# Another order of the second block's projections and another hand-written plan of turns

## The chip, the cores and the metric

The kernel runs on one core of one Trainium2 chip. The metric is the device time of one execution, in microseconds (us). A run of the kernel before takes 1793.36 us (median of three, 1793.31 to 1794.03).

## The reference

Input x is 256 tokens of 1024 float32 values. The first block is two layers, each of a half-weighted SwiGLU feed-forward, a hybrid mixer (gated convolution and a gated linear recurrence) and another feed-forward, with layer norms. It is not touched. The second block is this, cut to what matters (`_hgrn2` is a gated linear recurrence of 4 heads of 128, `_dsa_attention` an attention of 8 heads of 64):

```python
h = _rms(x, norm1_g) * (1 + sc1) + sh1
z = h @ w_in
rq, rf, ri, rg, aq, ak, av, iq, ik, iw = jnp.split(z, IN_OFFSETS, axis=-1)
rec = _hgrn2(rq, rf, ri, rg, lb, rec_out_g)
aq, ak = _rms(aq by head, q_norm_g), _rms(ak by head, k_norm_g)
ik = _layernorm(ik, idx_k_norm_g, idx_k_norm_b)
att = _rms(_dsa_attention(aq, ak, av, iq, ik, iw, rel_bias), attn_out_g)
x = x + g1 * (concatenate([rec, att]) @ w_out)
x = x + g2 * _hier_moe(...)
```

In the attention, each query's 64 best keys are selected by an index score, the sum over 8 index heads of iw * relu(iq . ik), and only these keys (of admissible chunks) enter the softmax, with a relative position bias.

## The kernel before, in words

**Weights.** All weights come from memory as 1 MB blocks, each of two halves of 128x1024 float32. ScalarE casts a half to a high part (L195) and VectorE subtracts to get the low part (L196); TensorE multiplies in three products, high by high, high by low and low by high. So each half costs one instruction on ScalarE and one on VectorE before TensorE can take it. There are six split buffers. `spend` (L257) is called after each half: it releases the half, lets the next one be split and calls `tick`. At most three halves are split ahead of the one in use.

**Projections.** The loop over `ZSEQ` (L32) makes z piece by piece. RF, RQ and IQ (forget gates, recurrence queries, index queries) are four halves of 24 matmuls with 256 columns (L317 to L319), IK (index keys and index weights) is one such half. AK, RG, AV and RI (attention keys, recurrence gate, attention values, recurrence values) are four halves of 12 matmuls with 512 columns (L348). AQ is made ahead of the loop. The order before is RF, RQ, IK, IQ, AK, RG, AV, RI.

**Everything else in between.** The rest of the block's first part is written as Python generators in three queues. `tick` (L251) takes the next entry of `PLAN` (L34): its three digits say how many steps are taken from each queue at that point. There are two ticks in a half (one in the middle, one at its end), some before the loop, and after the loop `tick` goes on until the second queue is empty, then three output halves follow with three ticks each. A step issues instructions to all engines; each engine runs its own in order, so a step issued early stands ahead of the splits issued later on the same engine.
- First queue: `prepare` (constants, the bounds of the forget gate, L952), `index_keys` (norm and transposition of the index keys), `index_scores` (L985: six chunks of scores, then eight rounds that take the eight largest values each, L1010 and L1011, then a threshold, L1013), and `attention` (L1159).
- Second queue: `decay` (L1016, forget gates and running sums), `levels` (L1078) and `recurrence` (L1107).
- Third queue: `qk_norm` (L1141): square sums, then a multiply by the root for each of four tiles and for the two query tiles a multiply by the gain on GpSimd (L1151), then transposes.

`levels` works through seven distances: `level_in` (L1055) subtracts running sums (L1068, L1070, on VectorE or GpSimd by the bits of `LVS`), takes the exponential on ScalarE and multiplies (L1075 by the bits of `LVD`, L1076 on VectorE); `merge_level` (L1032) makes two tiles of matmuls (L1037) and VectorE copies them under a mask (L1038), which gives their PSUM bank back. Two buffers (`kd`, `qd`) take turns over the levels, so a level's input waits for the merge two levels before. `across` (L1041) is the last input, followed by a cross block (A01).

`attention` loads the bias as two 512 KB transfers on GpSimd's queue (L1166), the first into the buffer of aq, the second into that of iq; it adds the threshold result to it (`bias`), and for each head makes logits (L1192), a maximum and exponentials, transposes of the weights with copies (`values`, L1207) and products with the values (L1212 to L1214). Its norm ends in transposes (L957) after a multiply (L1252).

PSUM: `mm_tile` gives one of four banks in turn. When the projection named by `ATT_AT` (L33) begins, `attention` is queued and two of the four become its output banks; from then on two are left for everything else. `acc` banks are separate.

**Turns before, by the plan.** Scans of the forget gates come in RQ, the levels from IK to RG (the last merge and the cross block at RG's first half), scores in AK and RG, seven of the eight selection rounds at one turn in RG (digit 7 of "702"), square sums and norms in RG, transposes of queries and keys in AV, the bias from RI's first half, most of attention in RI and behind it.

Of the kernel before, what the change touches and what calls it, by code (L numbers as in the profile page):

```python
# [28 lines left out]
NSTAG = 5  # L29
OFF_B, OFF_C, OFF_V, OFF_XR, OFF_YR, OFF_G = 0, 1024, 2048, 3072, 4096, 5120  # L30
Z_RQ, Z_RF, Z_RI, Z_RG, Z_AQ, Z_AK, Z_AV, Z_IQ, Z_IK = 0, 512, 1024, 1536, 2048, 2560, 3072, 3584, 4096
ZSEQ = (Z_RF, Z_RQ, Z_IK, Z_IQ, Z_AK, Z_RG, Z_AV, Z_RI)  # L32
ATT_AT = Z_RI  # L33
PLAN = (  # L34
# [3 lines left out]
).split()  # L38
LAG_V, LAG_P = 1, 3
LVS = 161  # L40
# [28 lines left out]
BIG = 99.0  # L69
# [10 lines left out]
def weight_order():  # L80
# [42 lines left out]
    order.extend(("zt", Z_AQ, q) for q in range(4))  # L123
    for o in ZSEQ:
        if o == Z_IK:
# [99 lines left out]
def kernel(ctx, tc, x, blocks, vecs, lnrows, consts, rows, bias_w, wr, out):  # L225
# [675 lines left out]
    def t4(shape, dt=F32, name="t4"):  # L901
        return p2.tile(shape, dt, tag="t4", bufs=4, name=name)
# [256 lines left out]
    def attention(mix, oa):  # L1159
# [4 lines left out]
        for i in range(2):  # L1164
            b = t4([128, 4, 256], name="braw")
            nc.gpsimd.dma_start(b, bass.AP(tensor=scr.tensor, offset=scr.offset + 2048 * i + 127,  # L1166
                                           ap=[[4095, 128], [512, 4], [1, 256]]))
            braw.append(b)

        def bias(h):  # L1170
            b = braw[h // 4][:, h % 4]
            bm = p2.tile([128, 384], F32, tag="bm", bufs=2, name="bm")
            eng = nc.vector if BSD >> h & 1 else nc.gpsimd
            eng.tensor_add(bm[:, 0:128], b[:, 128:256], idx[:, 0:128])
            eng.tensor_add(bm[:, 128:384], b, idx[:, 128:384])
            bts[h] = bm
# [112 lines left out]
    ready = set()  # L1289
    for off in ZSEQ:  # L1290
        if off == ATT_AT:
            turn_[1] = False
            oa = [o_tile("oatt") for _ in range(2)]
            bg.append(attention(mix, oa))
# [520 lines left out]
```

## Time and profile before

| what | us |
|---|---|
| median of the runs | 1793.36 |
| the profiled execution, its own time | 1794.38 |
| its span in the trace | 1792.5 |
| TensorE busy | 1722.5 (96%) |
| VectorE busy | 1340.1 (75%) |
| ScalarE busy | 1036.5 (58%) |
| GpSimd busy | 62.0 (3%) |

The span is from the first to the last recorded instruction; 1.9 us of the profiled execution lie around it. Its mean granted TensorE clock is 0.991 of full speed. Times in rows are us from the start of the span unless they are marked ns. "Busy" counts instructions in execution; shares are averages over very different stages. The projections of the second block's loop run from 1298.7 us on; at 1448.4 us the part after them begins.

### The profile page before, as it was taken

Reading aid. Unit: us, or ns where it says so; the run is one execution under the profiler, and the core shown is the slowest. Engines: PE = TensorE matmul, PEld = TensorE weight load, DVE = VectorE, ACT = ScalarE, POOL = GpSimd, SP = SyncE. Lnnn points to the kernel's source line nnn. Section 1 sums busy time; section 2 is a strip of 40 time slices with the busy share of each in tenths; the row PEclk is TensorE's granted clock in tenths of the full one; section 3 lists DMA queues with packets and bytes.
Section 4 is the critical chain, followed back from the end, with each engine's and each line's share of the span. In section 5 each row is a group of like instructions: output and inputs, shape, how many; then the busy total and the mean of one; then the engine's idle time right before and its main releaser. Section 6 shows DMA issues by size and latency. Waiting matters only on the chain. (4 is left out here: it accounts for less than half of the span.)

```text
span 1792.5 us, 25724 instructions
## 1 busy us (share of the span) xinstructions
PE 1722.5 (96%) x10089; PEld 1501.5 (84%) x10089; DVE 1340.1 (75%) x1913; ACT 1036.5 (58%) x1500; POOL 62.0 (3%) x74
## 2 busy tenths in 40 slices
PE   7999999999999999999999998999899879999998
PEld 6888799999788878887999997888698667877876
DVE  5777878756767786778787557566778778998996
ACT  5655575644555555555756444555466547777774
POOL 0000000000000000000000000000114120000000
PEclk9999999999999999999999999999999989999999
DMA  8566645554557665666455545655352357988983
GB/s 321 206 252 246 233 171 185 188 192 161 223 208 260 239 244 188 250 246 246 176 188 185 187 169 202 244 190 180 119 188 92 126 197 294 352 315 332 348 317 131
DMA packets 56384, 394.12 MB, mean 220 GB/s; under 512 B 6424, under 2 KB 6728, under 8 KB 9920
## 3 DMA queue, kind: packets, MB, share of 16 engines
q1 hardware_dynamic: 52416, 375.94, 56.9%
q0 software_dynamic: 3264, 15.74, 2.6%
q8 instruction: 81, 1.33, 0.3%
q10 hardware_dynamic: 576, 0.74, 0.1%
q14 instruction: 47, 0.39, 0.1%
HBM read 391.30 MB, written 3.19 MB: 220 GB/s over the span
## 5 line engine op out<-in xcount | busy, mean ns | idle before, releaser
L196 DVE TENSOR_TENSOR split<-raw,split 128x1024 fp32r<-128x1024 f32 x611 | 735.7, 1226 | 260.0 <-ACT split L195 257.6
L195 ACT CAST split<-raw 128x1024 fp32r<-128x1024 f32 x611 | 627.9, 1048 | 99.1 <-PE acc L384 54.2
L329 PE MATMUL mmo<-xT,split 128*128 128x512 f32 x640 | 230.0, 399 | 0.0
L329 PE MATMUL mm<-xT,split 128*128 128x512 f32 x640 | 229.3, 398 | 0.0
L384 PE MATMUL acc<-split,ht 128*128 128x512 f32 x816 | 199.5, 392 | 4.1 <-ACT ht L311 3.5
L1544 PE MATMUL hp<-split,xg 128*128 128x512 f32 x768 | 187.7, 398 | 0.8 <-DVE split L196 0.8
L384 PEld LDWEIGHTS acc<-split,ht 128*128 128x128 f32 x816 | 147.9, 188 | 38.7 <-ACT ht L311 4.8
L330 PE MATMUL mmo<-xT,split 128*128 128x256 f32 x640 | 179.7, 281 | 0.0
L330 PE MATMUL mm<-xT,split 128*128 128x256 f32 x640 | 179.6, 281 | 0.0
L1544 PEld LDWEIGHTS hp<-split,xg 128*128 128x128 f32 x768 | 142.9, 188 | 34.7 <-DVE split L196 1.1
L317 PE MATMUL mm<-xT,split 128*128 128x256 f32 x600 | 169.9, 283 | 0.0
L319 PE MATMUL mm<-xT,split 128*128 128x256 f32 x600 | 169.8, 283 | 0.0
L318 PE MATMUL mm<-xT,split 128*128 128x256 f32 x600 | 169.8, 283 | 0.0
L329 PEld LDWEIGHTS mmo<-xT,split 128*128 128x128 f32 x640 | 120.3, 188 | 29.6
L329 PEld LDWEIGHTS mm<-xT,split 128*128 128x128 f32 x640 | 120.2, 188 | 29.1
L330 PEld LDWEIGHTS mm<-xT,split 128*128 128x128 f32 x640 | 120.8, 189 | 2.0
L330 PEld LDWEIGHTS mmo<-xT,split 128*128 128x128 f32 x640 | 120.9, 189 | 0.7
L317 PEld LDWEIGHTS mm<-xT,split 128*128 128x128 f32 x600 | 115.1, 192 | 0.3
L318 PEld LDWEIGHTS mm<-xT,split 128*128 128x128 f32 x600 | 115.1, 192 | 0.3
L319 PEld LDWEIGHTS mm<-xT,split 128*128 128x128 f32 x600 | 115.1, 192 | 0.0
L317 PE MATMUL mmo<-xT,split 128*128 128x256 f32 x336 | 95.2, 283 | 0.0
L318 PE MATMUL mmo<-xT,split 128*128 128x256 f32 x336 | 95.1, 283 | 0.0
(464 smaller groups left out, 2792.5 us busy)
## 6 DMA issues: line engine op xcount, KB each, us to landing
raw<-in_w_dram SPq DMA_DIRECT2D x328, 1024.0 KB, 4.9
spare<-in_w_dram SPq DMA_DIRECT2D x27, 1024.0 KB, 4.8
lng<-in_ln_dram POOLq DMA_DIRECT2D x6, 1024.0 KB, 5.0
raw<-in_w_dram SPq DMA_DIRECT2D x4, 512.0 KB, 10.6
scr<-brow POOLq DMA_DIRECT2D x1, 2048.0 KB, 8.8
cb<-in_row_dram POOLq DMA_DIRECT2D x3, 512.0 KB, 7.1
norm<-mrow POOLq DMA_DIRECT2D x2, 512.0 KB, 4.8
braw<-scr POOLq DMA_DIRECT2D x2, 512.0 KB, 5.0
```

Of the source, the lines that this page charges most:

```text
L195: self.nc.scalar.copy(t[:, 0], r)
L196: self.nc.vector.tensor_sub(t[:, 1], r, t[:, 0].bitcast(F32))
L317: nc.tensor.matmul(ps, w[:, 0, k], xT[:, 0, k], start=(k == 0), stop=False)
L318: nc.tensor.matmul(ps, w[:, 0, k], xT[:, 1, k], start=False, stop=False)
L319: nc.tensor.matmul(ps, w[:, 1, k], xT[:, 0, k], start=False, stop=(k == 7))
L329: nc.tensor.matmul(both, w[:, 0, k], xT[:, :, k], start=(i == 0), stop=False)
L330: nc.tensor.matmul(ps[:, 256:512], w[:, 1, k], xT[:, 0, k], start=False, stop=(i == 7))
L384: nc.tensor.matmul(acc[T][n], a[:, hx], half[:, hw, n * 512:n * 512 + 512], start=(first and hx == 0 and hw == 0), stop=(last and hx == 1))
L1544: nc.tensor.matmul(ps, xgs[g][:, hx, k], wv[:, hw, kk], start=(k == 0 and hx == 0 and hw == 0), stop=(k == 7 and hx == 1))
```

## The change

The order `ZSEQ` becomes IK, IQ, RF, RQ, AK, RG, AV, RI. `ATT_AT` becomes AV, so attention's output banks are taken, and it is queued, one projection sooner. `PLAN` has other entries: the norm of the index keys is issued in IQ, the six score chunks at one turn each in RF with the first selection round, the other rounds at one turn each in RQ and AK, scans in RQ, the levels' inputs and merges from AK to the first half of AV (the last merge and the cross block at the end of AV's first half), square sums and norms in RG, transposes from RG's end to AV's second half, the bias transfers at the middle of AV's second half, attention from AV's third half on. In `attention` a `yield BIG` stands between the bias transfers and the first use of what they load, so that a turn lies between them. The weights' order in memory follows `ZSEQ`. No instruction is added or taken out.

```diff
--- before.py
+++ after.py
@@ -29,12 +29,12 @@
 NSTAG = 5
 OFF_B, OFF_C, OFF_V, OFF_XR, OFF_YR, OFF_G = 0, 1024, 2048, 3072, 4096, 5120
 Z_RQ, Z_RF, Z_RI, Z_RG, Z_AQ, Z_AK, Z_AV, Z_IQ, Z_IK = 0, 512, 1024, 1536, 2048, 2560, 3072, 3584, 4096
-ZSEQ = (Z_RF, Z_RQ, Z_IK, Z_IQ, Z_AK, Z_RG, Z_AV, Z_RI)
-ATT_AT = Z_RI
+ZSEQ = (Z_IK, Z_IQ, Z_RF, Z_RQ, Z_AK, Z_RG, Z_AV, Z_RI)
+ATT_AT = Z_AV
 PLAN = (
-    "100 000 511 010 000 001 022 000 101 010 010 010 010 010 100 030 110 000 111 011 000 010 100 001 121 "
-    "200 301 000 200 030 140 000 000 012 340 010 000 002 004 110 011 001 003 820 000 100 702 200 013 013 "
-    "150 000 000 001 001 240 101 200 100 001 112 320 531 420 415 202 001 101 000 401 100 000 110"
+    "100 100 000 000 000 000 000 100 000 000 100 100 000 000 000 100 100 100 100 100 100 100 010 110 100 "
+    "010 110 100 100 000 010 100 010 110 100 120 000 020 002 021 001 022 000 022 001 021 001 021 111 000 "
+    "100 100 100 100 100 100 100 200 100 200 100 200 220 210 220 220 100 000 100 100 100 100 100 100"
 ).split()
 LAG_V, LAG_P = 1, 3
 LVS = 161
@@ -1166,6 +1166,7 @@
             nc.gpsimd.dma_start(b, bass.AP(tensor=scr.tensor, offset=scr.offset + 2048 * i + 127,
                                            ap=[[4095, 128], [512, 4], [1, 256]]))
             braw.append(b)
+        yield BIG
 
         def bias(h):
             b = braw[h // 4][:, h % 4]
```

## Rows read from the trace of the kernel before

**Rows 1.** windows of the span: busy us per engine (x instructions), granted clock, DMA share, GB/s
```profile
1298.70:1448.40 149.70, 138.54 (x875) 119.37 (x874) 116.97 (x217) 89.38 (x147) 43.43 (x44) 0.98 0.36 126
1298.70:1324.00 25.30, 25.30 (x211) 25.23 (x210) 17.11 (x26) 17.89 (x21) 6.39 (x5) 1.00 0.59 214
1298.70:1400.60 101.90, 94.46 (x640) 85.17 (x639) 83.98 (x157) 60.63 (x81) 30.95 (x26) 0.98 0.39 137
1420.30:1437.70 17.40, 14.83 (x109) 12.13 (x107) 9.63 (x21) 12.65 (x33) 4.21 (x5) 1.00 0.18 66
0.00:1298.70 1298.70, 1261.17 (x7762) 1123.17 (x7763) 927.00 (x1375) 708.16 (x1076) 13.85 (x29) 1.00 0.58 211
1448.40:1792.50 344.10, 322.77 (x1455) 258.92 (x1453) 296.11 (x324) 238.94 (x279) 4.73 (x2) 0.98 0.79 296
```

**Rows 2.** waits of PE, 1298.7 to 1448.4: us in total, times, longest
```profile
PE acc L348 <- DVE split L196: 5.1, 1, 5.1
PE oatt L1212 <- ACT pT L1207: 2.0, 1, 2.0
PE mm L957 <- ACT ikw L1298: 1.2, 1, 1.2
```

**Rows 3.** windows of 10 us around the long wait, columns as in Rows 1
```profile
1390.00:1400.00 10.00, 4.93 (x20) 3.75 (x19) 9.59 (x38) 2.67 (x3) 1.74 (x3) 0.85 0.37 109
1400.00:1410.00 10.00, 10.00 (x37) 7.15 (x36) 8.70 (x15) 4.39 (x8) 1.15 (x2) 0.81 0.71 269
```

**Rows 4.** timeline of DVE, selection rounds and a split: start, us, engine, line
```profile
1387.39 0.29 DVE L1010 MAX8 mx<-idx 128x8 f32<-128x128 f32 x1
...
1388.84 0.28 DVE L1010 MAX8 mx<-idx 128x8 f32<-128x128 f32 x1
...
1397.52 1.22 DVE L196 TENSOR_TENSOR split<-raw,split 128x1024 fp32r<-128x1024 f32 x1
1398.65 0.29 DVE L1010 MAX8 mx<-idx 128x8 f32<-128x128 f32 x1
```

**Rows 5.** timeline of PE, the same stretch, in brackets the idle time before
```profile
1398.79 2.50 PE L348 MATMUL acc<-split,xT 128*128 128x512 f32 x5 [5.07 <-DVE split L196]
```

**Rows 6.** groups of DVE, 1298.7 to 1400.6: busy us, mean ns, idle before
```profile
L196 DVE TENSOR_TENSOR split<-raw,split 128x1024 fp32r<-128x1024 f32 x25 | 29.9, 1324 | 8.3 <-ACT split L195 8.3
L1003 DVE SCALAR_TENSOR_TENSOR idx<-relu,iw,idx 128x256 f32<-128x256 f32 (+1 forms) x14 | 7.7, 549 | 0.6
...
L952 DVE TENSOR_SCALAR lbc<-lbc 128x4 f32<-128x4 f32 x1 | 3.3, 3339 | 0.0
...
L976 DVE SCALAR_TENSOR_TENSOR ikd<-ikd,imv,row 128x128 f32<-128x128 f32 x2 | 0.7, 352 | 0.1
```

**Rows 7.** groups of POOL, the same stretch
```profile
L1068 POOL TENSOR_TENSOR kd<-bs 128x512 f32<-128x512 f32 x5 | 8.6, 1722 | 23.0 <-DVE bs L1026 18.9 <-PE mmo L1037 3.2 <-PE mm L1037 0.9
...
L1151 POOL TENSOR_TENSOR aq<-aq,gqk 128x512 f32<-128x512 f32 x2 | 3.8, 1882 | 13.3 <-DVE aq L1149 13.3
```

**Rows 8.** timeline of POOL and DVE, two subtractions at once
```profile
1324.06 2.02 POOL L1068 TENSOR_TENSOR kd<-bs 128x512 f32<-128x512 f32 x1
...
1325.10 1.53 DVE L1070 TENSOR_TENSOR qd<-bs 128x512 f32<-128x512 f32 x1
```

**Rows 9.** timeline of PE, merge matmuls and projection halves
```profile
1360.95 1.13 PE L1037 MATMUL mmo<-qd,kd 128*128 128x128 f32 x8
...
1362.73 7.07 PE L348 MATMUL acc<-split,xT 128*128 128x512 f32 x30
```

**Rows 10.** timeline of PE, the end of the stage
```profile
1429.03 1.33 PE L1115 MATMUL mm<-vv,atT 128*128 128x128 f32 x10
...
1436.00 1.23 PE L957 MATMUL mm<-ident,rs 128*128 128x128 f32 x8
...
1444.52 1.23 PE L957 MATMUL mm<-ident,at 128*128 128x128 f32 x8 [1.15 <-DVE at L1252]
```

**Rows 11.** page, part 6: KB each, median us from issue to landing
```profile
braw<-scr POOLq DMA_DIRECT2D x2, 512.0 KB, 5.0
```

## The prediction, made before the changed kernel was run

> **What bounds the kernel now.** I read the windows of the span first. Outside 1298.7 to 1448.4 us the change only reorders which weights are loaded; before it TensorE is busy 1261.2 of 1298.7 us, behind it 322.8 of 344.1 [rows 1]. I take both as unchanged. The stage in between holds all projections that are reordered, up to the experts: 149.7 us with TensorE busy 138.5, so 11.2 idle [rows 1]. The waits of TensorE name most of that: 5.1 for one split on VectorE, 2.0 for an attention copy, 1.2 for the index keys' evacuation [rows 2], and 1.15 at the end for the attention norm [rows 10]. The long one has a plain cause on the timeline. Seven of the eight selection rounds are issued at one turn; a round takes 1.45 us (1387.39 to 1388.84), and the split that TensorE needs stands among them at 1397.52 [rows 4]. TensorE goes on at 1398.79 after 5.07 us [rows 5]. Around it the granted clock is 0.85 and 0.81 in two windows of 10 us [rows 3]; in the second, 0.19 x 10 / 0.5 = 3.8 us were at the lower level, 1.2 GHz, and with the 1.2 us from 1398.79 on about 5.0 us of matmuls ran there, which costs half of that, 2.5 us. So **at most 13.7 us (11.2 + 2.5) are to be had**, and TensorE alone at full clock needs 138.5 - 2.5 = 136.0 us. VectorE is nearly as full: 84.0 us busy of the first 101.9, but only 17.1 of the first 25.3 [rows 1], and 9.59 of ten before the long wait [rows 3].
>
> **The change part by part.** No instruction is added or taken out, so the sum is 136.0 us plus the waits of the new order.
>
> Projections. Index keys and queries go first. Their scores (six chunks) and one selection round then fall into the forget projection, where VectorE had only splits; the other rounds get a turn each. The 5.07 us wait and the 1.2 us wait for the index keys are gone: in the new order a projection half stands between evacuation and use. The cost is elsewhere: scans, the levels (subtractions, exponentials, multiplies, merges), square sums and norms, which began in IK and IQ, now all lie from RQ to the first half of AV.
>
> VectorE's load there. Up to the first half of AV it has 84.0 us of before, less two splits that are not due yet: 81.7 (a split takes 1.13 us start to start [rows 4]). Of this, done by the end of the forget projection: ten splits 11.3, the bounds 3.3, the index keys' six small lines, at most 0.7 each and by their number some 2.6, the scores 7.5, of which 7.7 is the larger group's own busy sum with small overlaps [rows 6], and one round 1.45: together 26.2. That leaves 55.5 us. At its densest here VectorE shows 9.59 us of ten [rows 3]; I take 0.972, between that and full, and the 55.5 take 57.1.
>
> TensorE's load there. A projection half of the four later kinds is 12 matmuls; 30 took 7.07 us with some 0.2 of the last one's tail, so 2.75 [rows 9]. A half of RQ is 24 matmuls at 0.12 us, from 211 in 25.3 us [rows 1], so 11.5 for four. A merge pair is 1.8 us, from 1360.95 to 1362.73 [rows 9]. RQ 11.5; AK 11.0 + 3 merges = 16.4; RG 11.0 + 4 merges + four transposes 0.5 (eight took 1.23 with their tail [rows 10]) = 18.7; first half of AV 2.75 + one merge + the cross block 0.9 + eight transposes 1.05 = 6.5. Together 53.1. **VectorE lacks 4.0 us.** The queue is in order, so it can't be put off: merge copies, which free the matmul banks, stand behind it. In the old order the first 25.3 us gave VectorE 8.2 idle us too, but only the splits could use them.
>
> GpSimd's queue. In the norm turns two multiplies by the gain stand ahead of the sixth level's subtraction. They took 1.88 us each and a subtraction 1.72 [rows 7]. VectorE's multiply for that level waits for it, and behind it on VectorE stand the copies that give banks back. Attention takes its two output banks before AV, one projection sooner, so only two banks are left there and TensorE's transposes wait too. Bounds: 0 if the multiplies are long done, 5.5 for the three in a row (3.8 + 1.7), 8.5 with the exponential, the multiply and the copy behind them (1 us each, an estimate from the split's 1.22 for twice the elements [rows 4]). I take 5.5: the norm steps come two turns before the level, and VectorE, which feeds them, is late by then, so that is nearest to a full queue.
>
> Clock. A wait of about that length ended in half speed before [rows 3, 5]; the wait of 2.0 did not, its window being granted 1.00 [rows 1, 2]. I take 2.5 again, bounds 0 and 5.0.
>
> [...]
>
> Two engines on one port. A subtraction on VectorE took 1.53 us while one on GpSimd ran 2.02 [rows 8]: it ended 0.55 after the other. Such waiting is in the busy rows above, so I add nothing; if the new order meets less of it, VectorE's 57.1 falls.
>
> The Trainium skill ("SBUF — State Buffer", SBUF: two separate sides) calls the shared pair an exclusive lock, so that one of the two is blocked for the whole of the other. By that rule alone each GpSimd operation put beside a full VectorE lengthens it by its own time, and a shortage of 4.0 is the least there is; the trace agrees for this pair.
>
> Bias transfers. The two 512 KB loads are issued at the middle of the second AV half, and the new yield puts one half of projection (2.75 us) between them and their first use; a load lands in 5.0 us [rows 11]. So VectorE may wait 0 to 2.3 us. Splits up to three halves ahead (8 us) cover it, if VectorE has made them; if not, the splits behind the bias add are late. I take 0. On SP's queue the weight loads only change order, with the DMA engines 0.36 busy [rows 1]: 0.
>
> The end. Two waits of 2.0 and 1.15 are there now, 3.2 [rows 2, 10]. The new plan shares more of attention with RI, so the drain is shorter and the recurrence's first product comes sooner; its chain to the transposes lasted 7.0 us (1429.03 to 1436.00 [rows 10]) with more matmuls between than will be left, some 5 us: 2.0 more wait. The attention norm's root comes behind a split: one split later, 1.1. Sum 6.3, bounds 3.2 and 8.
>
> **Sum:** 136.0 + 4.0 + 5.5 + 2.5 + 6.3 = 154.3 us for the stage, 4.6 longer. The profiled execution took 1794.4 us (span 1792.5 and 1.9 around it), 1.0 above the median of 1793.4; I put the 4.6 on the median: **1798.0**. What a measurement of this kernel can tell from no change is about 0.2%, 3.6 us.
>
> **Rivals.** *VectorE keeps up* (faster). The 55.5 hold waiting on GpSimd's operations (a mean of 1324 ns for a split against 1.22 [rows 4, 6]; the 1.53 above); if the new order has 3 us less of it, the shortage and the jam behind it vanish: 136.0 + 6.3 = 142.3, 7.4 shorter, 1786.0. For it: VectorE's idle time at the start is used at last, and the 5.07 us wait has a cause that the change takes out. Against: 57.1 to 53.1 has no slack.
> *No jam at GpSimd* (about the same). The shortage is spread over short waits and the clock stays up: 136.0 + 4.0 + 6.3 = 146.3, 3.4 shorter, 1790.0. It decides whether the gain multiplies are done before the sixth level's subtraction is issued.
> *Each level waits* (much slower). If from AK on each of six merges is late by 1 us, since subtraction, exponential and multiply cross three engines within two turns, 6 us come on top: 160.3, 10.6 longer, 1804.0. The old plan gave the levels the same two turns or fewer, but beside a VectorE with room.
> *The plan doesn't do what it says*: were selection still bunched, the 5.07 would stay. The new plan's entries give one round a turn, so under 1 in 20, counted with the same.
>
> **How the numbers follow.** Forecast 0.42 (1794 to 1803 by its bounds), VectorE keeps up 0.22, no jam 0.20, each level waits 0.16. Faster by over 0.2%: 0.22. Same: 0.20. Slower: 0.58. The range leaves out half of the fastest case and the far end of the slowest: 1786 to 1807.
>
> **What would show it.** Right: no wait by a split in AV's last half; VectorE near full from RQ to AV; TensorE's waits in RG and AV on merge copies or the levels' multiplies, together some 9 us; a granted clock under 1 in AV. Wrong: TensorE without gaps from RF to RI, or VectorE with idle time in AK and RG that no GpSimd row explains, or a change before 1298 or in the experts.

## The result, and the profile after

The changed kernel takes 1808.55 us (median of four, 1807.09 to 1813.88) against 1793.34 for the kernel before on the same chip: a ratio of 1.0086, 95% interval 1.0073 to 1.0098. It is **15.2 us slower**. The forecast said slower by 4.6 and a range that ends at 1807; the sign was right, the size a third of what came.

The profiled execution took 1809.52 us by its own time, with a span of 1807.7. The busy time of the engines on its page:

```profile
PE 1736.0 (96%) x10089; PEld 1512.8 (84%) x10089; DVE 1338.5 (74%) x1913; ACT 1036.5 (57%) x1500; POOL 63.2 (3%) x74
```

VectorE, ScalarE and GpSimd are as busy as they were, within 2 us; TensorE is 13.5 us more busy with the same matmuls, 6.2 of them in the stage (144.8 in place of 138.5 [rows 1]), where its clock fell more often. The stage from the first matmul of the reordered projections to the first one behind them, and its three parts, in windows (columns as in the rows of before: PE, PEld, DVE, ACT, POOL busy us, granted clock, DMA share, GB/s). The part in the middle goes from the end of RF to the cross block, which follows the last merge:

```profile
1300.74:1463.38 162.64, 144.75 (x873) 124.36 (x872) 115.04 (x217) 88.52 (x146) 42.96 (x42) 0.95 0.34 121
1300.74:1334.30 33.56, 33.56 (x251) 30.96 (x250) 19.66 (x37) 18.54 (x26) 2.18 (x3) 1.00 0.52 184
1334.30:1404.00 69.70, 57.64 (x345) 51.24 (x344) 62.37 (x120) 37.24 (x50) 27.02 (x21) 0.91 0.28 98
1404.00:1463.38 59.38, 53.54 (x281) 42.16 (x281) 33.01 (x61) 32.74 (x71) 13.76 (x19) 0.96 0.32 112
1463.38:1807.70 344.32, 324.59 (x1455) 260.70 (x1453) 296.24 (x324) 239.47 (x280) 5.93 (x5) 0.97 0.78 293
```

The stage takes 162.6 us, where it took 149.4 from the same matmul to the same matmul (1298.96 to 1448.36), so 13.2 of the 15.2 us are in it. What follows takes 344.3 us, as in [rows 1]. The rest is ahead of the stage: here it starts at 1300.7 us, and in the other executions profiled below, which do the same work up to there, at 1297.2 to 1304.0. That spread is not the change's, and so the experiments below are read by the length of the stage as well as by the ratios. One execution of the run "new order, other plan", of 4330.51 us, counts as slow and is left out of its ratio.

TensorE is idle 17.9 us in the stage (11.2 before). Its waits, which answer to [rows 2]:

```profile
PE mmo L1037 <- DVE qd L1076: 5.5, 3, 3.2
PE mm L1037 <- DVE atT L1038: 3.8, 1, 3.8
PE mmo L957 <- DVE atT L1038: 2.7, 1, 2.7
PE mm L957 <- DVE rs L1129: 1.9, 1, 1.9
PE mm L957 <- DVE at L1253: 1.8, 1, 1.8
PE mm L1115 <- ACT vv L1316: 1.4, 1, 1.4
PE oatt L1213 <- ACT pT L1208: 0.8, 1, 0.8
```

The 5.1 us for a split and the 1.2 us for the index keys are gone. In their place stand the multiplies of the levels (L1076), and masked copies (L1038) that give a bank back late. How late they are the timelines of TensorE and VectorE show together. TensorE first (line L1037 is a merge, L957 a transpose):

```profile
1380.42 1.05 PE L1037 MATMUL mmo<-qd,kd 128*128 128x128 f32 x8
...
1386.40 1.13 PE L1037 MATMUL mmo<-qd,kd 128*128 128x128 f32 x8 [1.26 <-DVE qd L1076]
...
1391.16 0.63 PE L957 MATMUL mmo<-ident,aq 128*128 128x128 f32 x4 [2.74 <-DVE atT L1038]
...
1400.42 1.86 PE L1037 MATMUL mm<-qd,kd 128*128 128x128 f32 x7 [3.84 <-DVE atT L1038]
```

VectorE over the same time:

```profile
1386.89 1.29 DVE L1149 TENSOR_TENSOR aq<-aq,ss 128x512 f32<-128x512 f32 x2
1388.10 2.28 DVE L196 TENSOR_TENSOR split<-raw,split 128x1024 fp32r<-128x1024 f32 x1
1390.31 0.71 DVE L1038 COPY_PREDICATED atT<-mask,mmo 128x512 f32<-128x512 uint8 x1
...
1395.01 1.91 DVE L1149 TENSOR_TENSOR ak<-ak,ss 128x512 f32<-128x512 f32 x2
1396.85 2.28 DVE L196 TENSOR_TENSOR split<-raw,split 128x1024 fp32r<-128x1024 f32 x1
1399.05 0.71 DVE L1038 COPY_PREDICATED atT<-mask,mmo 128x512 f32<-128x512 uint8 x1
```

The merge of 1380.42 is copied at 1390.31, 8.8 us after its matmuls ended, the one of 1386.40 at 1399.05, 11.5 us after. Just ahead of each copy stand two norm multiplies and a split, lengthened by GpSimd: a split that takes 1.22 us alone [rows 4] takes 2.28 beside GpSimd's operations, the first of these beside the first split, the last beside the second:

```profile
1387.66 3.85 POOL L1151 TENSOR_TENSOR aq<-aq,gqk 128x512 f32<-128x512 f32 x2 [1.95 <-DVE aq L1149]
1391.47 1.04 POOL L1068 TENSOR_TENSOR kd<-bs 128x512 f32<-128x512 f32 x1
...
1396.33 1.71 POOL L1052 TENSOR_TENSOR kd<-kd,ks 128x512 f32<-128x512 f32 x1
```

The Trainium skill ("SBUF — State Buffer", SBUF: two separate sides) tells of an exclusive lock on the pair of ports that VectorE and GpSimd share; the 2.28 us agree with its direction, and the first split still ended, at 1390.38, before GpSimd's two multiplies did, at 1391.51. VectorE itself is not busy for 7.3 us of the middle part; 4.5 of that are waits for exponentials of the levels:

```profile
DVE qd L1076 <- ACT qd L1073: 2.9, 3, 1.4
DVE kd L1075 <- ACT kd L1072: 1.6, 1, 1.6
```

The 1.6 us go back to GpSimd: that exponential needs the subtraction of 1391.47 above, which starts when the two multiplies by the gain end. ScalarE's timeline:

```profile
1392.54 0.63 ACT L1072 ACTIVATE kd<-kd 128x512 f32<-128x512 f32 x1 [3.84 <-POOL kd L1068]
```

And the granted clock falls again, further than in [rows 3]:

```profile
1390.00:1400.00 10.00, 5.42 (x20) 4.17 (x20) 8.43 (x10) 6.24 (x10) 8.50 (x8) 0.78 0.34 121
1400.00:1410.00 10.00, 9.58 (x47) 8.92 (x48) 3.81 (x6) 4.15 (x7) 4.99 (x4) 0.71 0.64 220
```

### The profile page after: what moved, and what is told of

Its sections match the earlier page's. It is cut to its first block, busy times and chain, and to the rows that moved or that the text cites. A ratio compares the mean times of both kernels' runs of the same rounds, so it can differ in the third digit from the quotient of the medians.

```text
span 1807.7 us, 25712 instructions
## 1 busy us (share of the span) xinstructions
PE 1736.0 (96%) x10089; PEld 1512.8 (84%) x10089; DVE 1338.5 (74%) x1913; ACT 1036.5 (57%) x1500; POOL 63.2 (3%) x74
## 5 line engine op out<-in xcount | busy, mean ns | idle before, releaser
L330 PE MATMUL mmo<-xT,split 128*128 128x256 f32 x640 | 179.7, 281 | 0.0
L330 PE MATMUL mm<-xT,split 128*128 128x256 f32 x640 | 179.6, 281 | 0.0
L317 PE MATMUL mm<-xT,split 128*128 128x256 f32 x568 | 160.9, 283 | 0.0
L319 PE MATMUL mm<-xT,split 128*128 128x256 f32 x568 | 160.8, 283 | 0.0
L318 PE MATMUL mm<-xT,split 128*128 128x256 f32 x568 | 160.7, 283 | 0.0
L329 PEld LDWEIGHTS mm<-xT,split 128*128 128x128 f32 x640 | 120.2, 188 | 29.1
L330 PEld LDWEIGHTS mm<-xT,split 128*128 128x128 f32 x640 | 120.8, 189 | 2.0
L317 PEld LDWEIGHTS mm<-xT,split 128*128 128x128 f32 x568 | 109.0, 192 | 0.3
L318 PEld LDWEIGHTS mm<-xT,split 128*128 128x128 f32 x568 | 109.0, 192 | 0.3
L319 PEld LDWEIGHTS mm<-xT,split 128*128 128x128 f32 x568 | 108.9, 192 | 0.0
L317 PE MATMUL mmo<-xT,split 128*128 128x256 f32 x368 | 104.9, 285 | 0.0
L318 PE MATMUL mmo<-xT,split 128*128 128x256 f32 x368 | 104.1, 283 | 0.0
## 6 DMA issues: line engine op xcount, KB each, us to landing
raw<-in_w_dram SPq DMA_DIRECT2D x4, 512.0 KB, 10.6
```

What stands on the lines that cost most here:

```text
L317: nc.tensor.matmul(ps, w[:, 0, k], xT[:, 0, k], start=(k == 0), stop=False)
L318: nc.tensor.matmul(ps, w[:, 0, k], xT[:, 1, k], start=False, stop=False)
L319: nc.tensor.matmul(ps, w[:, 1, k], xT[:, 0, k], start=False, stop=(k == 7))
L329: nc.tensor.matmul(both, w[:, 0, k], xT[:, :, k], start=(i == 0), stop=False)
L330: nc.tensor.matmul(ps[:, 256:512], w[:, 1, k], xT[:, 0, k], start=False, stop=(i == 7))
```

## The experiments

A stage length below is from the first matmul of the reordered projections to the first matmul behind the stage (L450), and "to the cross block" is from the same start to its first matmul; the changed kernel has 162.6 and 103.3 us. Ratios are against the kernel before, whose medians beside these runs were 1793.3 to 1796.0; so runs are compared by their ratios, and 0.001 of the ratio is 1.8 us. The length of the stage scatters too: up to the cross block "root sooner" issues the same instructions as the changed kernel and comes there 0.9 us later.

| run | median us | ratio, 95% interval | stage us | to the cross block |
|---|---|---|---|---|
| changed kernel | 1808.55 | 1.0086 (1.0073 to 1.0098) | 162.6 | 103.3 |
| one round | 1803.04 | 1.0047 (1.0030 to 1.0064) | 157.5 | 96.8 |
| banks | 1807.37 | 1.0076 (1.0059 to 1.0092) | 163.8 | 102.9 |
| gain on VectorE | 1806.65 | 1.0075 (1.0056 to 1.0095) | 160.6 | 100.9 |
| fillers | 1807.67 | 1.0081 (1.0064 to 1.0098) | 162.8 | 104.2 |
| half as many fillers | 1806.42 | 1.0061 (1.0044 to 1.0079) | 161.5 | 103.4 |
| index work sooner | 1803.24 | 1.0053 (1.0036 to 1.0070) | 157.4 | 100.6 |
| old order, rounds spread | 1795.29 | 1.0009 (0.9999 to 1.0019) | 149.5 | |
| new order, other plan | 1787.55 | 0.9964 (0.9944 to 0.9984) | 140.0 | 80.1 |
| old order, other plan | 1789.49 | 0.9980 (0.9970 to 0.9990) | 144.1 | |
| root sooner | 1808.01 | 1.0076 (1.0055 to 1.0097) | 163.0 | 104.2 |

**One round.** Is it VectorE's load that makes TensorE wait?

```diff
-        for _ in range(8):
-            for T, o, nk in ((0, 0, 128), (1, 128, 256)):
+        for k in range(8):
+            for T, o, nk in ((0, 0, 128), (1, 128, 256))[0:2 if k == 0 else 0]:
```

> The changed kernel with seven of the eight selection rounds left out (its output is then another one), so VectorE has some 10 us (7 x 1.45) less to do between the first quarter of RQ and AK. Theory V (VectorE, in order and short of time, makes TensorE wait wherever the queue's delay reaches it): the waits of merges in AK (1.0 and 3.2 us) go and with the second its half-speed stretch (some 1.5 us): 6 to 8 us faster than the changed kernel, the waits in AV stay as they are. Theory B (the waits come from having only two matmul banks from AV on) and theory G (they come from GpSimd's queue): AK's waits have nothing to do with either, and AV's stay: under 2 us faster.

The stage is 5.1 us shorter, which is less than the 6 to 8 expected; the cross block comes 6.5 us sooner, and the ratios differ by 0.0039, some 7 us. The waits of TensorE, those lines that answer to the theory:

```profile
PE mm L1037 <- DVE atT L1038: 3.8, 1, 3.8
PE mmo L957 <- DVE atT L1038: 2.7, 1, 2.7
...
PE mmo L1037 <- DVE qd L1076: 0.8, 1, 0.8
```

Of the 5.5 us for the levels' multiplies 0.8 are left, and the two waits on copies are as they were. That is theory V's case; neither the banks nor GpSimd's multiplies had anything to do with what went.

**Banks.** Is it that attention takes two of four banks a projection sooner?

```diff
         if off == ATT_AT:
-            turn_[1] = False
-            oa = [o_tile("oatt") for _ in range(2)]
+            oa = []
             bg.append(attention(mix, oa))
+        if off == Z_RI:
+            turn_[1] = False
+            oa.extend(o_tile("oatt") for _ in range(2))
```

> The changed kernel, but attention takes its two output banks only before RI, so that four matmul banks serve in AV as they did before the change. Theory B: the two waits on masked copies in AV (2.7 and 3.8 us) and their half-speed stretches (some 4 us) go: 7 to 10 us faster than the changed kernel. Theory V: the copies are late on VectorE by about 10 us; with more banks TensorE meets the same delay one step later: 0 to 3 us faster, the wait only moves to another line. Theory G: 0 to 2.

The ratio is 0.0010 lower, some 1.8 us, the stage 1.1 longer: nothing that could be told from no difference. The 3.8 us wait on a copy is down to 0.8, and a 2.6 us wait on the evacuation of a transpose has come, while the copies ahead of the transposes cost 1.4:

```profile
PE mmo L1037 <- DVE qd L1076: 6.9, 4, 3.2
PE mmo L1037 <- ACT qT L1157: 2.6, 1, 2.6
...
PE mmo L957 <- DVE atT L1038: 1.4, 1, 1.4
```

Theory B falls. The early banks decide on which line the delay shows, not how long it is.

**Gain on VectorE.** Is it GpSimd's queue, for which the prediction had 5.5 us?

```diff
-                nc.gpsimd.tensor_tensor(sv, sv, gqk[:, None, :].to_broadcast([128, 8, 64]), op=ALU.mult)
+                nc.vector.tensor_tensor(sv, sv, gqk[:, None, :].to_broadcast([128, 8, 64]), op=ALU.mult)
```

> The changed kernel with the two multiplies by the query gain on VectorE instead of GpSimd, so that the sixth level's subtraction has nothing ahead of it on GpSimd; VectorE has two more multiplies of some 0.7 us. Theory G (the prediction's term of 5.5 us for GpSimd's queue): the waits in AV shrink by 4 us or more and the second half-speed stretch goes: 5 to 8 us faster. Theory V: VectorE gets 1.4 us more work in the stretch where it is short, and loses the contention with the two multiplies: between 2 us faster and 1.5 us slower.

2.0 us by the ratios, 2.0 in the stage: the far end of theory V and short of theory G. The two waits on copies in AV have become one of 4.9 us, and VectorE's wait of 1.6 for the exponential behind GpSimd's subtraction is gone.

So the queue that the prediction saw at GpSimd is there, but its two multiplies cost about 2 us net of the 1.4 that they bring VectorE, not 5.5.

**Fillers.** Is it the half clock? Idle matmuls were put where TensorE waits.

```diff
+            for _ in range(24 if n == 1 and T == 0 else 0):
+                nc.tensor.matmul(ps[:, 0:128], ks[:, 0, sl], qs[:, 0, sl], start=True, stop=True)
...
+            if off == Z_AV and q == 0:
+                for _ in range(28):
+                    nc.tensor.matmul(acc[0][0:32, 0:128], zero, ks[:, 0, 0:128], start=False, stop=False)
```

> The changed kernel with idle matmuls put in front of two waits: 24 ahead of the merge that waits 3.2 us in AK (into the bank that is overwritten behind them) and 28 that add zero times a key tile to AV's first sums, ahead of the merge that waits 3.8 us. They take some 2.6 and 3 us at full speed and lie inside the waits. Theory C (the part of the loss that the sum missed is TensorE's clock: after each wait of about 3 us it ran some 3 to 6 us at 1.2 GHz): the granted clock stays at 1.00 behind both, and the kernel is 3 to 5 us faster than the changed one, though it does more. Rival (the half speed does not come from the waits, or the loss is the waits alone): the same time or up to 1 us slower.

The clock stayed at full speed behind both, and the stage is as long as without. But this run can't tell the theories apart, since the fillers were too long: each is two records, and together they took 5.5 and 6.3 us, more than the waits of 3.2 and 3.8 that they were to fill:

```profile
1360.05 5.52 PE L1039 MATMUL mmo<-qs,ks 128*128 128x128 f32 x48
...
1394.74 6.30 PE L1283 MATMUL acc<-ks,zero 128*32 128x128 f32 x56
```

**Half as many fillers.** The same edit with 13 and 15 in place of 24 and 28.

> The first run with idle matmuls again, with about half as many (13 and 15), because they took 5.4 and 6.3 us there, longer than the waits of 3.2 and 3.8 us that they were to fill; here some 2.9 and 3.4 us. Theory C (the half speed behind the two waits costs time of its own): full speed stays, the merges start as early as in the changed kernel, and behind the last merge before the cross block TensorE is 3 to 4.5 us ahead: so much faster than the changed kernel. Theory V (VectorE sets the pace there; at full speed TensorE waits for it instead): behind the first of the two the next waits grow by what the clock gives; behind the second at most 2.5 us are gained, since VectorE has little left to do from there on: 0 to 2.5 us faster.

Now they fit. TensorE's timeline (L1039 and L1283 are the fillers, L1041 the merges, L1098 the cross block):

```profile
1359.70 3.06 PE L1039 MATMUL mmo<-qs,ks 128*128 128x128 f32 x26
1363.02 1.13 PE L1041 MATMUL mmo<-qd,kd 128*128 128x128 f32 x8 [0.26 <-DVE qd L1080]
...
1384.91 1.13 PE L1041 MATMUL mmo<-qd,kd 128*128 128x128 f32 x8 [2.05 <-DVE qd L1080]
...
1395.03 3.46 PE L1283 MATMUL acc<-ks,zero 128*32 128x128 f32 x30
1398.96 2.05 PE L1041 MATMUL mm<-qd,kd 128*128 128x128 f32 x16 [0.46 <-DVE atT L1042]
1401.89 1.13 PE L1098 MATMUL mm<-qd,kd 128*128 128x128 f32 x8 [0.88 <-DVE atT L1042]
```

The merge in AK starts 0.3 us after the fillers, at full speed, and what that gives is spent at the merge of 1384.91, which now waits 2.05 where it waited 1.26. The windows of this run, up to the cross block and behind it:

```profile
1298.48:1401.89 103.41, 95.23 (x650) 85.12 (x648) 84.45 (x157) 55.49 (x74) 27.60 (x24) 0.98 0.35 125
1401.89:1460.02 58.13, 52.94 (x281) 41.33 (x282) 32.67 (x61) 32.74 (x71) 14.40 (x20) 0.97 0.34 116
```

The cross block comes after 103.4 us, as in the changed kernel (103.3), with a granted clock of 0.98 in place of 0.94; behind it 58.1 us in place of 59.4. So theory C's 3 to 4.5 us are not there: up to the cross block TensorE at half speed costs nothing that shows beyond the scatter of a microsecond, as VectorE sets the pace, and at full speed TensorE waits instead. Nor is it shown to be exactly nothing, since VectorE's own busy time up to there was 84.5 us here and 82.0 in the changed kernel, for the same instructions. Behind the cross block the clock is worth 1.3 us: 0.8 between the cross block and the first logits (6.1 us in place of 6.9), the rest at the transposes ahead of the output (L957, 1449.54 in the changed kernel), which ran at full speed here.

The ratio fell by 0.0025, some 4.5 us, which taken alone is theory C's range; its interval still meets that of the changed kernel, and the stage, which holds all the fillers, is 1.1 us shorter.

**Index work sooner.** Only plan entries: two score chunks to a turn in RF's first half, the rounds moved up.

```diff
-    "100 100 000 000 000 000 000 100 000 000 100 100 000 000 000 100 100 100 100 100 100 100 010 110 100 "
-    "010 110 100 100 000 010 100 010 110 100 120 000 020 002 021 001 022 000 022 001 021 001 021 111 000 "
+    "100 100 000 000 000 000 000 100 000 000 100 100 000 000 000 200 200 200 100 100 100 200 110 110 100 "
+    "110 100 000 000 000 010 000 010 010 000 020 000 020 002 021 001 022 000 022 001 021 001 021 111 000 "
```

> The changed kernel with other plan entries for the index work alone: the six score chunks two to a turn in the first half of RF, so that selection ends near the end of RQ and not in AK. Theory V, refined (what is lost is VectorE's idle time in the first 33.6 us, where it was busy 19.7 us; what it does not do there it has to do where it is short): some 3 to 4 us of rounds move from AK into time that was idle, the waits of AK's first merges shrink, the pair in AV by about as much: the last merge comes 3 to 5 us sooner, and the whole is 2 to 5 us faster than the changed kernel. Rival (the levels wait by the length of their own chain over three engines, not for VectorE's time): the same within 1 us.

5.9 us by the ratios, 5.2 in the stage, a little over what was expected; the cross block comes 2.7 us sooner, under what was expected. Its three windows stand beside those of the changed kernel above:

```profile
1299.13:1332.70 33.57, 33.57 (x278) 32.32 (x277) 24.29 (x57) 20.41 (x28) 2.30 (x3) 1.00 0.44 164
1332.70:1399.70 67.00, 54.59 (x329) 46.76 (x327) 61.65 (x101) 37.36 (x49) 33.03 (x23) 0.95 0.34 127
1399.70:1456.53 56.83, 51.09 (x271) 39.44 (x271) 32.73 (x61) 30.66 (x69) 11.43 (x17) 0.97 0.31 100
```

VectorE does 24.3 us of work by the end of RF in place of 19.7, and the middle part is 2.7 us shorter. Of the 4.6 us that are done earlier only 0.7 are missing from VectorE's busy time there (61.7 for 62.4): the levels' multiplies took longer, beside a GpSimd that was busy 33.0 us of this part in place of 27.0. The larger group of the middle part, in the changed kernel and in this run:

```profile
L1076 DVE TENSOR_TENSOR qd<-qd,qs 128x512 f32<-128x512 f32 x7 | 6.3, 902 | 2.9 <-ACT qd L1073 2.9
L1076 DVE TENSOR_TENSOR qd<-qd,qs 128x512 f32<-128x512 f32 x7 | 8.3, 1189 | 2.7 <-ACT qd L1073 2.7
```

The rest of the gain is behind the cross block (56.8 in place of 59.4), where this run can't say why.

**Old order, rounds spread.** Was the long wait of the kernel before really to be had by spreading the rounds? One plan line of that kernel:

```diff
-    "200 301 000 200 030 140 000 000 012 340 010 000 002 004 110 011 001 003 820 000 100 702 200 013 013 "
+    "200 301 000 200 030 140 000 000 012 340 110 100 102 104 110 111 101 103 120 100 100 102 200 013 013 "
```

> The kernel before, order and everything else as it was, with one idea of the change alone: the selection rounds one to a turn instead of seven at one, with the scores some turns sooner. If the 5.07 us wait and the half speed behind it came from the bunching, all 7.6 us are to be had: 1786. Theory V says that the wait was VectorE's shortage showing at one place: the rounds that no longer stand before the one split stand before others and before the transposes of the norms; 0 to 2 us faster than the kernel before.

The ratio is 1.0009 (0.9999 to 1.0019): no gain at all, which is the lower end of what theory V gave. The 5.1 us wait is gone from the list; a wait of 2.1 on a copy ahead of a score chunk and one of 1.0 on the gain multiply (L1151) have come, beside those that were there:

```profile
PE mmo L993 <- DVE atT L1038: 2.1, 1, 2.1
```

The stage is as long as before (149.5), but not for the waits alone. TensorE is idle 8.8 us of it in place of 11.2, and what that gave went to the clock, which stayed low behind the wait of 2.1 us:

```profile
1365.37:1376.00 10.63, 10.63 (x32) 8.33 (x33) 8.87 (x20) 4.13 (x7) 0.43 (x1) 0.52 0.30 99
```

TensorE was busy for all of these 10.6 us and VectorE for 8.9, so here the half speed did not stand in for a wait while it lasted; what full speed would have given is not shown, as VectorE is busy for 24.4 of the next 25 us. So the 7.6 us were not to be had by this plan line. Whether the bunching by itself cost something, the run leaves open.

**New order, other plan.** The changed kernel with its order, its early banks and its yield, and only `PLAN` replaced.

```diff
+    "100 000 000 100 000 000 100 000 000 000 200 100 000 200 000 000 300 500 000 000 000 000 000 010 000 "
+    "000 000 000 000 130 040 010 020 010 140 000 000 000 000 003 041 000 000 001 010 200 001 000 200 000 "
+    "001 100 104 100 000 011 000 501 300 000 000 100 000 200 000 000 100 820 100 110 500 040 000 000"
```

> The changed kernel, its order and its early output banks kept, with other plan entries: all scores and two selection rounds in RF's first half, the levels from AK on in bunches, the last six rounds, the norms of keys and the transposes spread over AV and RI, where VectorE had been half idle, and most of attention behind RI. Theory V: the order is not to blame, the load between RQ and AV is; with some 12 us of VectorE's work moved behind the first half of AV the waits of 12 us there go, and part of it comes back behind RI, where TensorE has nothing but attention: 8 to 15 us faster than the changed kernel, at or below the one before. Rival (taking the banks and the index work early costs in itself): within 4 us of the changed kernel.

1787.55 us: by the ratios some 22 us faster than the changed kernel, and faster than the one before (0.9964, 0.9944 to 0.9984), more than was expected. The stage takes 140.0 us, 4 above the 136.0 of TensorE alone at full clock that the prediction had worked out. The windows, cut at RF's end and at the cross block:

```profile
1303.21:1443.25 140.04, 134.27 (x873) 117.78 (x872) 114.97 (x215) 87.58 (x144) 40.90 (x40) 0.99 0.40 141
1303.21:1336.90 33.69, 33.04 (x272) 32.00 (x271) 23.52 (x54) 20.61 (x29) 2.31 (x3) 1.00 0.43 157
1336.90:1383.30 46.40, 45.05 (x299) 40.36 (x298) 44.41 (x68) 30.05 (x39) 19.71 (x16) 1.00 0.38 137
1383.30:1443.25 59.95, 56.18 (x308) 45.42 (x307) 47.05 (x95) 36.92 (x78) 18.87 (x21) 0.97 0.39 134
```

VectorE has the same work, 115.0 us in all. In the changed kernel it lay 19.7, 62.4 and 33.0 in the three parts; here it lies 23.5, 44.4 and 47.0, as four selection rounds, the four norm multiplies and the transposes follow the cross block. In the middle VectorE is still 96% busy, and TensorE 97%. What waits are left are short:

```profile
PE oatt L1213 <- ACT pT L1208: 1.5, 2, 1.1
PE mmo L1037 <- DVE qd L1076: 1.3, 2, 0.7
```

**Old order, other plan.** The kernel before, only `PLAN` replaced.

```diff
+    "202 000 100 050 000 001 110 001 000 003 000 000 010 000 000 052 001 000 000 401 010 011 022 110 010 "
+    "413 010 111 001 001 030 100 200 010 100 200 100 000 013 321 000 000 000 102 431 120 221 000 100 300 "
+    "003 003 500 100 011 211 140 010 010 000 021 100 001 603 200 332 400 020 364 200 001 000 000"
```

> The kernel before with its own order and other plan entries: levels from IK on one to two turns, selection rounds in three places in AK and RG, the norms of keys and the transposes in AV, attention from RI's first half on. If the plan alone holds the waits, this beats both kernels: 3 to 10 us faster than the kernel before. If VectorE's shortage from 1340 us on can't be spread further, the same within 2 us.

0.9980 (0.9970 to 0.9990), 4 us by the medians, with a stage of 144.1 us. Its two long waits on TensorE are 3.2 us for a norm multiply ahead of the transposes and the 2.0 for the attention copy.

So a plan that spreads VectorE's work beats the kernel before in either order. Whether one order is better than the other these two plans don't tell.

**Root sooner.** One term of the prediction's tail by itself: the root of the attention norm one turn sooner.

```diff
-    "100 100 100 100 100 100 100 200 100 200 100 200 220 210 220 220 100 000 100 100 100 100 100 100"
+    "100 100 100 100 100 100 100 200 100 200 100 200 220 210 220 220 100 100 000 100 100 100 100 100"
```

> The changed kernel with the root of the attention norm issued one turn sooner, in front of the split of the second output half and not behind it. The prediction had a term of 1.1 us for that split. If it is right, the wait of 1.8 us ahead of the last transposes shrinks to some 0.7 to 1.1 and the time by as much; if the norm waits for something else, nothing moves.

The wait ahead of the transposes is gone. From the first output matmul to the transpose TensorE takes 7.2 us (1449.27 to 1456.47) in place of 8.8 (1450.86 to 1459.69 in the changed kernel).

The whole does not show it: the interval covers the changed kernel's ratio, and the stage of this execution was later by 0.9 us at the cross block already. The place gave 1.6 us; that the time moved is not shown.

## Why the prediction was wrong in size

**The frame held.** Nothing moved behind the stage, no instruction was gained or lost, the two waits of before were gone, TensorE's idle time was 17.9 us for a forecast of 15.8 (4.0 + 5.5 + 6.3), and the waits were of the kind that was looked for: levels' multiplies and masked copies in RG and AV, then the drain. They were 12.0 us for some 9, and 4.2 of them lay in AK, which had not been named. The bias transfers cost nothing, as said.

**The step that failed is the one that shares out VectorE's work**: "Of this, done by the end of the forget projection: [...] together 26.2. That leaves 55.5 us." The sum was right to 0.3 us: 81.7 were expected up to the cross block, and 19.7 + 62.4 = 82.0 were done. But only 19.7 were done by the end of RF, and 62.4 were left. VectorE was idle 13.9 of the first 33.6 us: score chunks came one to a turn, the first selection round (1.45 us) and the end of the scores (1.1) slipped out of RF, and the scores themselves were shorter (430 ns on the mean of the first twelve, for 549 [rows 6]). The 3.3 us of the forget bounds were no work of their own: here they are 2.4 us from 1299.58 on, with splits running beside them from 1299.92 on, and in the kernel before they lie beside splits too, so the prediction counted that time twice. Of this term I gave no bounds, so the range's upper end did not hold it either. "One round" took 7 rounds out and brought the cross block 6.5 us sooner; "new order, other plan" left VectorE 44.4 us in the middle, and the stage fell to 140.0. "Index work sooner" did 4.6 us earlier and won 5.2 in the stage, of which 2.7 up to the cross block.

**GpSimd's queue, 5.5 us:** the size nearly fits, and that is luck. VectorE stood still 7.3 us of the middle part (1.6 had been allowed for as gaps), 4.5 of these for the levels' exponentials. Of the 4.5, the 1.6 behind the subtraction of 1391.47 are the queue that was forecast; the 2.9 have no gain multiply ahead of them, and taking the gain multiplies off GpSimd gave 2. With VectorE's 62.4 the middle part is 62.4 + 7.3 = 69.7 us; the forecast had 53.1 + 4.0 + 5.5 + 2.5 = 65.1. That is 4.6 of the 8.3 us by which the stage was missed (162.6 for 154.3). The 6.9 us of VectorE's work that were not foreseen weigh so little only because the 2.5 for the clock were not due beside them.

**The clock, 2.5 us:** it fell far more often than forecast, and up to the cross block cost nothing that shows ("half as many fillers"), since it replaced waiting. The forecast added it to VectorE's shortage; two limits of the same stretch don't add up. Behind the cross block it was not in the sum, and it counts there: 1.3 us by that run. At 1450, where it fell behind three waits in a row (1.00 to 0.5 for some 3.5 us), TensorE waits 1.8 us for the attention norm on VectorE afterwards, so most of that stretch replaced waiting too. The Trainium skill's rule that an idle array falls to half rate ("TensorE: Matmul & The Clock Gate", Part 1) agrees with the direction of these rows; what it costs they decide.

**The end, 6.3 us:** the four waits of the drain are 5.9 us together (1.4, 0.8, 1.9, 1.8), as forecast, and the root's split had its price (1.1 expected, 1.6 seen at the place). Still the part behind the cross block took 59.4 us where 49.3 + 6.3 = 55.6 follow from the prediction; the clock explains 1.3 of these 3.8 us, the rest stays open.

**The rivals.** "VectorE keeps up" and "no jam" did not come. "Each level waits" was nearest by its time (1804.0) and not by its mechanism: three merges waited, 5.5 us in all, and not for the chain over three engines but for rounds and copies queued on VectorE; with seven rounds less, 0.8 were left. That the plan does what it says held, and was no help: the 5.1 us wait went, and "old order, rounds spread" shows that its going alone wins nothing.

## What to carry to other kernels

List the load of the second engine for each stretch between two points that the first must pass, and ask of every item when its inputs come; idle time ahead of that can't be filled by it, and work that moves out of it comes back as waits. A plan that gives one step a turn looks even and is not: what has to be even is the work that the turns issue, against the work that covers it, and here the best plan left the rounds and norms for where VectorE was half idle. Before a wait is priced as a gain, ask whether its place or its engine is to blame: an engine without slack shows its shortage on whichever line stands behind it. And work that is moved can change its length: in "index work sooner" the levels' multiplies, beside more of GpSimd's work, took back most of what had left their stretch.

## What the runs showed of the hardware that was not expected

A TensorE at half clock cost nothing that showed while VectorE set the pace: 103.4 us to the cross block with the two stretches at full speed, 103.3 without, where equal instructions scatter by 0.9. That is not so everywhere: in "old order, rounds spread" TensorE was busy through 10.6 us at a granted 0.52 and VectorE for 8.9 of them. The clock fell after waits as short as 2.7 us with another of 1.3 a few microseconds earlier, and at 1450 after waits of 1.4, 0.8 and 1.9 us, none of which alone had done it in the kernel before (2.0 us there, clock 1.00 [rows 1, 2]). A float32 matmul of 128 columns showed as two records and took some 0.22 us in a row of fillers: 24 of them took 5.4 us from their start to the next matmul.
